# A transformer block in fp32 by split matmuls: seven-product pairs in every FFN group, three hidden tiles parked in DRAM, and the delta rule's norm weight moved to the split

## The chip, the cores and the metric

The kernel runs on one core of one Trainium2 chip, as one launch. The metric is the device time of a launch in microseconds (us), the median of three runs. TensorE is called PE below, VectorE DVE, ScalarE ACT, GpSimd POOL and SyncE SP.

## The reference

One hybrid transformer block on 256 tokens of width 2048, in fp32:

```python
proj = x @ w_in                                   # q,k,v of both branches, z, gates
o_a = gated_delta_rule_chunked(...)               # 8 heads of 128
o_a = o_a * rsqrt(mean(o_a**2) + eps) * gdn_norm_w * silu(z)
o_b = dsa_sparse_attention(...)
merged = sigmoid(gate_a) * (o_a @ w_branch_a) + sigmoid(gate_b) * (o_b @ w_branch_b)
x = layer_norm(ALPHA * x + merged @ w_out, ln1_g, ln1_b)
h_gate, h_up = split(x @ w_ffn_in)                # 2 x 5632 columns
x = layer_norm(ALPHA * x + (silu(h_gate) * h_up) @ w_ffn_out, ln2_g, ln2_b)
```

`gdn_norm_w` has 128 entries, one for each position within a head.

## The kernel before

**Split matmuls.** Each fp32 matrix is split into a rounded part `hi` and a rest `lo`, and a product is three matmuls, hi*hi + hi*lo + lo*hi (`mm3`). Weights arrive as 512 KB chunks of 128 x 1024: SP loads a chunk into one of four `raw` tiles, ACT makes `hi` (line 80), DVE makes `lo` (line 82), and PE uses both (`chunk`). There are four tiles each of `raw`, `hi` and `lo`; a load, a cast or a subtraction waits until its tile was given free.

**Pairs.** In the gate groups, the FFN groups and the output projection, the contraction goes in pairs `q` of two chunks (256 rows), against 1024 columns and both token blocks. A plain pair (`plain_pair`) is 8 block products, 24 matmuls of 512 columns. A seven-product pair (`seven_pair`) multiplies the 2 x 2 blocks by a scheme with 7 products, so it is 21 matmuls. It needs sums of weight blocks (`wt`, lines 248 to 252) with their own hi and lo (`thi`, `tlo`, lines 237 and 238), sums of the activations (`forms`), and a second bank of four PSUM tiles (`wbank`), which is joined to the first one later (`sums_chain`, `seven_chain`). `GQ`, `FQ` and `WQ` are the tables of which pairs are of seven products: `GQ` for the four gate groups, `FQ` for the FFN groups, `WQ` for the two column halves of the output projection.

**FFN.** Group 0 (`wfi`) is done plainly. Groups 1 to 10 (8 pairs each) give 512 hidden features each; `hidden_chain` forms silu(gate)*up, transposes it on PE (line 1150) and splits it into the tiles `hH[i]`, `hL[i]`. Where the output projection treats its pairs by seven products, the chain also makes their `forms` and writes them to DRAM (`d_g`). A chain is a generator that yields the number of ticks (half pairs) until its next step; `tick()` runs after each half pair, so the yields set where its matmuls stand in PE's order.

**Order.** PE and SP execute in program order (`manual_schedule`), with weight chunks moved ahead by `LEAD`. DVE, ACT and POOL are put in order by the tile scheduler, by priority; each engine then executes in that fixed order, so an instruction that waits holds up all behind it. The tiles `hH[7]` to `hH[10]` and `hL[7]` to `hL[10]` lie where the FFN's `f_wraw`, `f_wt`, `f_thi` and `f_tlo` are, and the activations' forms lie in the place of `x1`. So groups 8 to 10, during which those tiles are filled and `x1` is read back, are plain.

**Output projection.** `group(0, ...)` and `group(1, ...)` go over 22 pairs each. At pair 2 of group 0 the last chains are run out (`finish`), and the pools for the seven-product tiles (`wraw`, `wt`, `thi`, `tlo`, `gt`) are opened where the activations lay.

**Other places.** `out_gate_chain` multiplies silu(z) by the norm weight on POOL (line 837). `block_xs` for `wbb` (branch b) takes its PSUM tiles from `acc`, as does the gate group after it.

Of the kernel before, what the change touches and what calls it, by code (L numbers as in the profile page):

```python
# [52 lines left out]
def block_kernel(ctx: ExitStack, tc: tile.TileContext, xT, x, cpack, onehot, relb, convw, alog, dtb, gnw,  # L53
# [941 lines left out]
    hH, hL = [], []  # L995

    def h_tiles(pool, n):
        for _ in range(n):
            i = len(hH)
            hH.append(pool.tile([P, 4, S], F32R, name=f"hH{i}", tag=f"hH{i}"))  # L1000
            hL.append(pool.tile([P, 4, S], F32R, name=f"hL{i}", tag=f"hL{i}"))

    h_tiles(hp_, 5)
# [101 lines left out]
    h_tiles(hp2, 2)  # L1105
# [27 lines left out]
    def hidden_chain(i, bank, v, std):  # L1133

        if v is None:
            v = [fv() for _ in range(4)]
            for tb in range(NTB):
                nc.scalar.activation(v[2 * tb], bank[2 * tb], AF.Silu)
                nc.vector.tensor_mul(v[2 * tb + 1], bank[2 * tb + 1], v[2 * tb])
        else:  # L1140
            for tb in range(NTB):
                g, u = v[2 * tb:2 * tb + 2]
                nc.vector.tensor_tensor(g, bank[2 * tb], g, op=OP.subtract if tb else OP.add)
                nc.scalar.activation(g, g, AF.Silu)
                nc.vector.tensor_add(u, bank[2 * tb + 1], u)
            for tb in range(NTB):
                g, u = v[2 * tb:2 * tb + 2]
                nc.vector.tensor_mul(u, u, g)
        yield 4 if i < NG else 2
        a = [quad(lambda o, f: nc.tensor.transpose(o, v[2 * tb + 1][:, f * P:(f + 1) * P], ident), std)  # L1150
             for tb in range(NTB)]
        ps = [p for p in (2 * i, 2 * i + 1) if p in WALL]
# [20 lines left out]
    for i in range(1, NG + 1):  # L1173
        if i > 7:
            h_tiles(hp2, 1)
        if i == 8:
            x1 = [rp.tile([P, D], F32, name=f"x1_{tb}", tag=f"x1_{tb}") for tb in range(NTB)]
            for tb in range(NTB):
                nc.gpsimd.dma_start(x1[tb], d_x1[tb])
# [160 lines left out]
def _arrays(i):  # L1340
# [13 lines left out]
    def paired(m):  # L1354
# [63 lines left out]
```

## Time and profile before

| | |
|---|---|
| median of 3 runs | 1478.28 us (1476.67 to 1478.88) |
| profiled execution, its own time | 1477.79 us |
| span of its instructions | 1476.0 us |
| PE busy | 1459.3 us (99%), 7191 matmuls |
| DVE busy | 1146.1 us (78%) |
| ACT busy | 766.5 us (52%) |
| POOL busy | 52.6 us (4%) |
| moved by DMA | 307.59 MB, 208 GB/s over the span |
| granted clock of TensorE | 0.998 |

The span runs from the first to the last instruction of the profiled execution; the time has 1.8 us around it. Matmuls overlap in the pipeline: a row's duration is longer than the distance to the next row's start, and the cost of one is that distance.

### The profile page before, as it was taken

What the parts mean: (1) busy time and instruction counts of PE and PEld (TensorE: products, weight loads), DVE (VectorE), ACT (ScalarE), POOL (GpSimd) and SP (SyncE); (2) the same over time, 40 slices, a digit from 0 to 9 for tenths busy, and PEclk for the clock granted to TensorE, in tenths of its full rate; (3) what the DMA queues carried; (4) which work ended last, traced back from release to release, by engine and by line L of the source; (5) the groups of instructions that cost most, each with busy time, mean ns of one, the idle gap of its engine ahead of it and who ended that gap; (6) DMA issues with size and microseconds to landing.
All of it is one profiled execution on the core that took longest, in us unless ns stands there. A gap on an engine that the chain in (4) does not pass through costs nothing.

```text
span 1476.0 us, 19311 instructions
## 1 busy us (share of the span) xinstructions
PE 1459.3 (99%) x7191; PEld 1226.0 (83%) x7191; DVE 1146.1 (78%) x1534; ACT 766.5 (52%) x932; POOL 52.6 (4%) x63
## 2 busy tenths in 40 slices
PE   9999999999999999999999999999999999999996
PEld 9888888888888888888878888888888888888885
DVE  6798985468488678776676889988895556999896
ACT  6765443446466456543445556555554444664560
POOL 0001010020010000000000000000000000000000
PEclk9999999999999999999999999999999999999999
DMA  8656584545556665558656566666676666877862
GB/s 295 193 153 198 179 193 152 158 129 158 168 185 215 199 213 187 186 185 299 227 187 207 184 234 216 218 216 236 227 255 220 200 209 224 303 262 244 322 217 87
DMA packets 92398, 307.59 MB, mean 208 GB/s; under 512 B 16448, under 2 KB 17512, under 8 KB 91280
## 3 DMA queue, kind: packets, MB, share of 16 engines
q1 hardware_dynamic: 80592, 283.36, 58.9%
q0 software_dynamic: 4672, 20.65, 4.0%
q10 hardware_dynamic: 7040, 2.36, 0.7%
q8 instruction: 56, 0.92, 0.3%
q14 instruction: 38, 0.31, 0.1%
HBM read 292.50 MB, written 13.83 MB: 208 GB/s over the span
## 4 chain that ended last, share of the span: by engine, by line
PE 95%; DVE 2%; DMA 1%; ACT 1%; issue 1%; SPq 0%; POOLq 0%; DVEq 0%; ACTq 0%
PE acc L142 10%; PE acc L205 10%; PE acc L206 10%; PE acc L204 10%; PE aux L205 8%; PE aux L206 8%; PE aux L204 8%; PE acc L164 7%; PE acc L163 7%; PE acc L162 7%; PE acc L145 5%; PE aux L669 1%; DMA raw<-in_win_dram 1%; DVE lo L82 1%; ACT hi L80 1%
## 5 line engine op out<-in xcount | busy, mean ns | idle before, releaser
L82 DVE TENSOR_TENSOR lo<-raw,hi 128x1024 fp32r<-128x1024 f32 (+1 forms) x421 | 514.8, 1228 | 240.2 <-ACT hi L80 237.1
L80 ACT CAST hi<-raw 128x1024 fp32r<-128x1024 f32 (+1 forms) x421 | 437.7, 1046 | 483.6 <-PE acc L164 125.3
L142 PE MATMUL acc<-X,hi 128*128 128x512 f32 x640 | 203.7, 400 | 0.0
L204 PE MATMUL acc<-hi,X 128*128 128x512 f32 x388 | 151.6, 391 | 0.5 <-DVE s_vT L971 0.5
L206 PE MATMUL acc<-hi,X 128*128 128x512 f32 x388 | 151.0, 389 | 0.0
L205 PE MATMUL acc<-lo,X 128*128 128x512 f32 x388 | 151.0, 389 | 0.0
L145 PEld LDWEIGHTS acc<-X,lo 128*128 128x128 f32 x640 | 120.2, 188 | 28.3
L204 PE MATMUL aux<-hi,X 128*128 128x512 f32 x340 | 132.9, 391 | 0.0
L206 PE MATMUL aux<-hi,X 128*128 128x512 f32 x340 | 132.4, 389 | 0.0
L205 PE MATMUL aux<-lo,X 128*128 128x512 f32 x340 | 132.3, 389 | 0.0
L162 PE MATMUL acc<-hi,X 128*128 128x512 f32 x320 | 127.1, 397 | 0.0
L145 PE MATMUL acc<-X,lo 128*128 128x256 f32 x640 | 126.0, 278 | 0.0
L164 PE MATMUL acc<-hi,X 128*128 128x512 f32 x320 | 124.7, 390 | 0.0
L163 PE MATMUL acc<-lo,X 128*128 128x512 f32 x320 | 124.6, 389 | 0.0
L142 PEld LDWEIGHTS acc<-X,hi 128*128 128x128 f32 x640 | 97.5, 189 | 2.0 <-ACT hi L80 0.7
L204 PEld LDWEIGHTS acc<-hi,X 128*128 128x128 f32 x388 | 72.8, 188 | 15.9 <-DVE s_vT L971 1.0
L206 PEld LDWEIGHTS acc<-hi,X 128*128 128x128 f32 x388 | 72.8, 188 | 15.1
L205 PEld LDWEIGHTS acc<-lo,X 128*128 128x128 f32 x388 | 72.9, 188 | 15.0
L206 PEld LDWEIGHTS aux<-hi,X 128*128 128x128 f32 x340 | 63.8, 188 | 13.3
L205 PEld LDWEIGHTS aux<-lo,X 128*128 128x128 f32 x340 | 63.8, 188 | 13.1
L204 PEld LDWEIGHTS aux<-hi,X 128*128 128x128 f32 x340 | 63.8, 188 | 13.0
L164 PEld LDWEIGHTS acc<-hi,X 128*128 128x128 f32 x320 | 60.1, 188 | 12.7
(518 smaller groups left out, 2562.6 us busy)
## 6 DMA issues: line engine op xcount, KB each, us to landing
raw<-in_wfg_dram SPq DMA_DIRECT2D x143, 512.0 KB, 4.0
raw<-in_wws_dram SPq DMA_DIRECT2D x80, 512.0 KB, 3.8
raw<-in_wfo_dram SPq DMA_DIRECT2D x69, 512.0 KB, 4.6
raw<-in_wgt_dram SPq DMA_DIRECT2D x53, 512.0 KB, 3.6
raw<-in_win_dram SPq DMA_DIRECT2D x37, 512.0 KB, 3.7
raw<-in_wo_dram SPq DMA_DIRECT2D x32, 512.0 KB, 4.3
wraw<-in_wfo_dram SPq DMA_DIRECT2D x19, 512.0 KB, 5.0
gt<-d_g SPq DMA_DIRECT2D x19, 512.0 KB, 6.6
```

The lines of the kernel that those rows point to most:

```text
L80: nc.scalar.copy(hi, raw)
L82: nc.vector.tensor_sub(lo, raw, hi.bitcast(F32))
L142: nc.tensor.matmul(pss[c], hv[:, kk, cs[c]], X2[k // 4][:, k % 4], start=(k == 0), stop=False, skip_group_check=True)
L145: nc.tensor.matmul(pss[c][:, :S], lv[:, kk, cs[c]], xh[:, k, :], start=False, stop=(k == KT - 1), skip_group_check=True)
L162: nc.tensor.matmul(ps, xh, hv[:, kk], start=(k == 0), stop=False)
L163: nc.tensor.matmul(ps, xh, lv[:, kk], start=False, stop=False)
L164: nc.tensor.matmul(ps, xl, hv[:, kk], start=False, stop=(k == 2 * n - 1))
L204: nc.tensor.matmul(o, sh, hi, start=first, stop=False)
L205: nc.tensor.matmul(o, sh, lo, start=False, stop=False)
L206: nc.tensor.matmul(o, sl, hi, start=False, stop=last)
L669: nc.tensor.matmul(o, l, r, start=True, stop=True)
```

## The change

- The tables: `FQ` gives each FFN group but the first three seven-product pairs, (2, 4, 6), and all of the groups 1 to 10; `GQ` gives the first gate group a third one, pair 2; `WQ` has 10 and 8 pairs in place of 11 and 8, at other places.
- The hidden tiles of groups 0, 1 and 2 go through one pair of tiles (`pass`) to DRAM (`d_h`) and are read back by SP during group 0 of the output projection (`FETCH`), whose rows of `wfo` are put in another order, groups 3 to 10 first, then 1, 2 and 0. `x1` is written to DRAM by SP in place of POOL, somewhat later, and read back by SP at pairs 15 to 18 in place of group 8 of the FFN.
- `hidden_chain` copies both transposed tiles to SBUF on ACT, splits from there, and waits three ticks in all groups (before: four, and two in the last).
- The norm weight is a [128, 1] operand, applied where the transposed delta-rule output is split; the multiplication on POOL is gone.
- The last `wbb` block takes PSUM tiles of `aux`.

```diff
-WQ = ((2, 4, 6, 8, 9, 11, 13, 14, 16, 18, 19), (3, 5, 7, 8, 10, 12, 13, 15))
-GQ = ((4, 6), (2, 4, 6), (2, 4, 6), (2, 4, 6))
+WQ = ((2, 4, 6, 8, 9, 11, 12, 16, 17, 19), (3, 5, 7, 8, 10, 12, 13, 16))
+GQ = ((2, 4, 6),) * 4
-FQ = {1: (4, 6), 2: (4, 6), 3: (3, 4, 6), 4: (4, 6), 5: (3, 4, 6), 6: (4, 6), 7: (3, 4, 6)}
+FQ = ((4, 6), *[(2, 4, 6)] * 9)
+OUT_AT = (8, 9, 10)
+FETCH = (5, 7, 9, 10, 13, 14)
...
-        nc.gpsimd.tensor_tensor(s_rv.rearrange("p a h d -> p (a h) d"), s_rv.rearrange("p a h d -> p (a h) d"),
-                                bc(gnw_t[:, None, :], [P, NTB * H, P]), op=OP.mult)
...
-                split(oh_[:, hs, tb * P:(tb + 1) * P], ol_[:, hs, tb * P:(tb + 1) * P], a)
+                nc.scalar.activation(oh, a, AF.Copy, scale=gnw_t[:, 0:1])
+                nc.vector.scalar_tensor_tensor(ol, a, gnw_t[:, 0:1], oh.bitcast(F32), op0=OP.mult, op1=OP.subtract)
...
-        for tb, ps in enumerate(block_xs([wbb[j, k] for k in range(4)], oh_, ol_)):
+        for tb, ps in enumerate(block_xs([wbb[j, k] for k in range(4)], oh_, ol_, ps_aux if j == 3 else ps_acc)):
...
+    def put_out(i, hl):
+        for j, t in enumerate(hl):
+            nc.gpsimd.dma_start(d_h[i, j], t.rearrange("p k t -> p (k t)").bitcast(F32))
+    def fetch(i, j):
+        t = (hH, hL)[j][i]
+        nc.sync.dma_start(t.rearrange("p k t -> p (k t)").bitcast(F32), d_h[i, j])
...
-        nc.gpsimd.dma_start(d_x1[tb], x1[tb])
...
     def f_forms_chain():
         yield "x1"
+        for tb in range(NTB):
+            yield 2
+            nc.sync.dma_start(d_x1[tb], x1[tb])
...
-        yield 4 if i < NG else 2
+        yield 3
         a = [quad(lambda o, f: nc.tensor.transpose(o, v[2 * tb + 1][:, f * P:(f + 1) * P], ident), std)
              for tb in range(NTB)]
-        ps = [p for p in (2 * i, 2 * i + 1) if p in WALL]
-        if ps:
-            hq = fp.tile([P, 512], F32, name="hq", tag="hq", bufs=1)
-            nc.scalar.copy(hq, a[1])
+        hq = v[::2]
+        with tc.high_priority(offset=LEAD // 2):
+            for tb in range(NTB):
+                nc.scalar.copy(hq[tb], a[tb])
...
-            split(hH[i][:, :, ts], hL[i][:, :, ts], v4(a[tb]))
+            split(hl[0][:, :, ts], hl[1][:, :, ts], v4(hq[tb]))
+        if i < 3:
+            put_out(at, hl)
...
+            if not g and q in FETCH:
+                fetch(OUT_AT[0] + FETCH.index(q) // 2, FETCH.index(q) % 2)
+            if not g and 15 <= q < 19:
+                c, tb = divmod(q - 15, 2)
+                cs = slice(c * 1024, c * 1024 + 1024)
+                nc.sync.dma_start(x1[tb][:, cs], d_x1[tb, :, cs])
```

How the order of instructions moves, at three places. Lines in the changed kernel's rows are some two to twenty higher.

ACT's order at the start of the output projection, before: `hH_10448` is the tile of the last FFN group (its input `acc` are the transposes), `wraw` the first seven-product pair's weights.

```order
L1138 ACTIVATE v<-acc 128x512 x2
L80 CAST hi<-raw 128x1024
L195 CAST hH_10448<-acc 128x4x128 x2
L237 CAST hi<-wraw 128x1024
L237 CAST hi<-raw 128x512
L237 CAST thi<-wt 128x1024
```

The same place in the changed kernel.

```order
L1158 ACTIVATE v<-v 128x512
L82 CAST hi<-raw 128x1024
L1158 ACTIVATE v<-v 128x512
L1169 COPY v<-acc 128x512 x2
L197 CAST hH_10512<-v 128x4x128 x2
L239 CAST hi<-wraw 128x1024
L239 CAST hi<-raw 128x512
L239 CAST thi<-wt 128x1024
```

Before the first cast of `wraw` stand four instructions that depend on the transposes, where there were two; the transposes themselves stand behind 36 matmuls of the output projection in PE's order, where it was 24.

DVE's order in an FFN group with three seven-product pairs, before, around pairs 3 and 4: `fg` and `gs` are the forms of the group before, `f_wt` and `f_tlo` the weight sums.

```order
L238 TENSOR_TENSOR lo<-f_wraw,hi 128x1024
L252 TENSOR_TENSOR f_wt<-f_wt,raw 128x512
L269 TENSOR_TENSOR fg<-hq 128x2x128
L238 TENSOR_TENSOR lo<-raw,hi 128x512
L270 TENSOR_TENSOR fg<-acc,fg 128x2x128
L271 TENSOR_TENSOR fg<-hq,acc 128x2x128
L272 TENSOR_TENSOR fg<-acc,fg 128x2x128
L82 TENSOR_TENSOR lo<-raw,hi 128x1024 x2
L196 TENSOR_TENSOR gs<-fg,gs 128x2x512
L238 TENSOR_TENSOR f_tlo<-f_wt,f_thi 128x1024 x2
```

The same place in the changed kernel, around pair 4.

```order
L240 TENSOR_TENSOR lo<-f_wraw,hi 128x1024
L198 TENSOR_TENSOR hL_6126<-v,hH_6125 128x4x128
L271 TENSOR_TENSOR fg<-v 128x2x128
L240 TENSOR_TENSOR lo<-raw,hi 128x512
L272 TENSOR_TENSOR fg<-v,fg 128x2x128
L273 TENSOR_TENSOR fg<-v 128x2x128
L253 TENSOR_TENSOR f_wt<-f_wt,f_wraw 128x512
L274 TENSOR_TENSOR fg<-v,fg 128x2x128
L254 TENSOR_TENSOR f_wt<-f_wt,raw 128x512
L240 TENSOR_TENSOR f_tlo<-f_wt,f_thi 128x1024
L198 TENSOR_TENSOR gs<-fg,gs 128x2x512
L240 TENSOR_TENSOR f_tlo<-f_wt,f_thi 128x1024
```

The first `f_tlo` of a pair now stands ahead of `gs` and of the plain chunks' `lo`, and a plain pair lies between any two seven-product pairs.

SP's order in group 0 of the output projection, changed kernel, pairs 15 to 18 (before, the same queue had only `wraw`, `raw` and `gt` here): `x_0`, `x_1` are the two token blocks of `x1`.

```order
L1280 DMA x_0_10620<-d_x_6110 128x1024
L80 DMA raw<-in_wfo_dram 128x1024 x2
L1280 DMA x_1_10621<-d_x_6110 128x1024
L233 DMA wraw<-in_wfo_dram 128x1024
L235 DMA raw<-in_wfo_dram 128x1024
L1217 DMA gt<-d_g 128x1024
L1280 DMA x_0_10620<-d_x_6110 128x1024
L233 DMA wraw<-in_wfo_dram 128x1024
L235 DMA raw<-in_wfo_dram 128x1024
L1217 DMA gt<-d_g 128x1024
L1280 DMA x_1_10621<-d_x_6110 128x1024
L80 DMA raw<-in_wfo_dram 128x1024 x2
```

Four loads of `x1` stand among the weights' loads here, and six of `d_h` do so at the pairs of `FETCH`.

## Rows read from the trace of the kernel before

**Rows 1.** The page: busy time of each engine, and the chain that ended last.

```profile
PE 1459.3 (99%) x7191; PEld 1226.0 (83%) x7191; DVE 1146.1 (78%) x1534; ACT 766.5 (52%) x932; POOL 52.6 (4%) x63
PE 95%; DVE 2%; DMA 1%; ACT 1%; issue 1%; SPq 0%; POOLq 0%; DVEq 0%; ACTq 0%
```

**Rows 2.** Timeline of PE, output projection's start: start, duration, instruction, idle before.

```profile
1235.31 0.39 PE L204 MATMUL aux<-hi,hH 128*128 128x512 f32 x1
...
1240.52 0.40 PE L206 MATMUL aux<-hi,hL 128*128 128x512 f32 x1
1240.76 1.04 PE L1150 MATMUL acc<-ident,v 128*128 128x128 f32 x8
...
1250.52 0.39 PE L204 MATMUL acc<-thi,gt 128*128 128x512 f32 x1
1251.16 0.50 PE L205 MATMUL acc<-tlo,gt 128*128 128x512 f32 x1 [0.25 <-DVE tlo L238]
```

**Rows 3.** Stretches between transposes: length, PE, PEld, DVE, ACT, POOL, clock, DMA, GB/s.

```profile
855.30:898.40 43.10, 43.10 (x197) 35.78 (x196) 39.31 (x47) 25.65 (x30) 1.05 (x2) 1.00 0.68 231
898.40:941.20 42.80, 42.65 (x193) 35.05 (x192) 38.89 (x46) 24.39 (x29) 1.06 (x2) 1.00 0.65 210
1113.10:1157.50 44.40, 44.40 (x202) 36.85 (x201) 24.56 (x25) 20.26 (x22) 1.05 (x2) 1.00 0.67 214
```

**Rows 4.** The same by whole groups: group 3 (three seven-product pairs), group 4 (two).

```profile
887.50:930.40 42.90, 42.75 (x192) 35.12 (x192) 41.28 (x49) 25.61 (x30) 1.06 (x2) 1.00 0.64 209
930.40:973.40 43.00, 43.00 (x195) 35.72 (x194) 36.91 (x44) 24.46 (x28) 1.05 (x2) 1.00 0.70 231
```

**Rows 5.** Timeline of DVE in group 3.

```profile
898.61 1.22 DVE L238 TENSOR_TENSOR f_tlo<-f_wt,f_thi 128x1024 fp32r<-128x1024 f32 x1
899.75 0.68 DVE L238 TENSOR_TENSOR lo<-raw,hi 128x512 fp32r<-128x512 f32 x1
900.35 1.22 DVE L248 TENSOR_TENSOR f_wt<-f_wraw,raw 128x1024 f32<-128x1024 f32 x1
...
906.42 0.41 DVE L271 TENSOR_TENSOR fg<-hq,acc 128x256 f32<-128x256 f32 x1
906.75 0.41 DVE L272 TENSOR_TENSOR fg<-acc,fg 128x256 f32<-128x256 f32 x1
```

**Rows 6.** Timeline of PE in group 3, pair 4.

```profile
911.38 0.39 PE L204 MATMUL acc<-f_thi,f_form 128*128 128x512 f32 x1
911.91 0.50 PE L205 MATMUL acc<-f_tlo,f_form 128*128 128x512 f32 x1
```

**Rows 7.** Timeline of PE, from branch b to the third gate group.

```profile
533.62 0.39 PE L206 MATMUL acc<-hi,X 128*128 128x512 f32 x1
534.56 0.50 PE L204 MATMUL acc<-hi,X 128*128 128x512 f32 x1 [0.55 <-DVE s_vT L971]
```

**Rows 8.** Timeline of ACT, output projection's start.

```profile
1241.39 1.08 ACT L195 CAST hH<-acc 128x512 fp32r<-128x512 f32 x2 [4.83 <-PE acc L1150]
1242.35 1.06 ACT L237 CAST hi<-wraw 128x1024 fp32r<-128x1024 f32 x1
```

**Rows 9.** Timeline of DVE, output projection's start.

```profile
1243.45 1.23 DVE L238 TENSOR_TENSOR lo<-wraw,hi 128x1024 fp32r<-128x1024 f32 x1
...
1249.88 1.23 DVE L238 TENSOR_TENSOR tlo<-wt,thi 128x1024 fp32r<-128x1024 f32 x1
```

**Rows 10.** Busy time by stretch of the output projection; the last two columns are DMA.

```profile
1260.00:1270.00 10.00, 10.00 (x46) 8.29 (x45) 9.83 (x10) 5.49 (x7) 0.00 (x0) 1.00 0.95 338
...
1370.00:1380.00 10.00, 10.00 (x45) 8.29 (x45) 8.28 (x10) 6.14 (x7) 1.06 (x2) 1.00 1.00 370
```

**Rows 11.** Waits from 1235 us on: in total, times, longest.

```profile
DVE wt L248 <- DMA raw<-in_wfo_dram: 3.5, 4, 1.9
```

**Rows 12.** Timeline of POOL, first gate group.

```profile
410.34 4.63 POOL L837 TENSOR_TENSOR s_rv<-s_rv,gnw 128x2048 f32<-128x2048 f32 x1 [83.01 <-ACT s_rv L836]
```

**Rows 13.** Busy time around that instruction.

```profile
400.00:425.00 25.00, 25.00 (x112) 20.70 (x111) 17.45 (x19) 13.95 (x14) 4.63 (x1) 1.00 0.62 198
```

More of the change, by code (lines that the diff above doesn't have):

```diff
@@ L891, in forms_chain @@
     def forms_chain(room):
-        for q in (4, 6, 2):
+        for q in (2, 4, 6):
             yield 1
@@ L994, in block_kernel, with h_tile, passing @@
     hp_ = fh.enter_context(tc.tile_pool(name="hp", bufs=1, side="left", reuse_waits="tile"))
[L995 to L1003, printed above, removed]
+    hH, hL = [None] * (FT // 4), [None] * (FT // 4)
+    def h_tile(pool, i):
+        hH[i], hL[i] = (pool.tile([P, 4, S], F32R, name=f"{hl}{i}", tag=f"{hl}{i}") for hl in ("hH", "hL"))
+    d_h = dr.tile([FT // 4, 2, P, 1024], F32, name="d_h")
+    def passing():
+        return [hp_.tile([P, 4, S], F32R, name="pass", tag=f"{hl}0") for hl in ("hH", "hL")]
+    def put_out(i, hl):
[4 more added lines that the diff above has]
+        nc.sync.dma_start(t.rearrange("p k t -> p (k t)").bitcast(F32), d_h[i, j])
+    h_first = passing()
+    for i in range(1, 5):
+        h_tile(hp_, i)
     l1 = ExitStack()
@@ L1098, in h_chain @@
         fs = slice(2 * j, 2 * j + 2)
-        split(hH[0][:, fs, ts], hL[0][:, fs, ts], a[:, :2 * P].rearrange("p (k t) -> p k t", k=2))
+        split(h_first[0][:, fs, ts], h_first[1][:, fs, ts], a[:, :2 * P].rearrange("p (k t) -> p k t", k=2))
+        if j and tb:
+            put_out(OUT_AT[2], h_first)
     block_xs_stag([wfi[0, k] for k in range(8)], xh, xl, ex,
@@ L1104, in block_kernel @@
     hp2 = fh.enter_context(tc.tile_pool(name="hp2", bufs=1, side="left", reuse_waits="tile"))
-    h_tiles(hp2, 2)
+    for i in (5, 6):
+        h_tile(hp2, i)
     f_home = {}
@@ L1120, in f_forms_chain @@
         yield "x1"
+        for tb in range(NTB):
+            yield 2
+            nc.sync.dma_start(d_x1[tb], x1[tb])
         t = [rp.tile([P, 2, 2, 4, P], F32R, name="f_form", tag=f"x1_{tb}") for tb in range(NTB)]
-        for i, q in enumerate((4, 6, 3)):
+        for i, q in enumerate((4, 2, 6)):
             yield 1
@@ L1133, in hidden_chain @@
     def hidden_chain(i, bank, v, std):
[L1135 to L1148, printed above, removed]
-        yield 4 if i < NG else 2
+        for tb in range(NTB):
+            g, u = v[2 * tb:2 * tb + 2]
+            nc.vector.tensor_tensor(g, bank[2 * tb], g, op=OP.subtract if tb else OP.add)
+            nc.scalar.activation(g, g, AF.Silu)
+            nc.vector.tensor_add(u, bank[2 * tb + 1], u)
+        for tb in range(NTB):
+            g, u = v[2 * tb:2 * tb + 2]
+            nc.vector.tensor_mul(u, u, g)
+        yield 3
         a = [quad(lambda o, f: nc.tensor.transpose(o, v[2 * tb + 1][:, f * P:(f + 1) * P], ident), std)
              for tb in range(NTB)]
-        ps = [p for p in (2 * i, 2 * i + 1) if p in WALL]
-        if ps:
-            hq = fp.tile([P, 512], F32, name="hq", tag="hq", bufs=1)
-            nc.scalar.copy(hq, a[1])
+        hq = v[::2]
+        with tc.high_priority(offset=LEAD // 2):
+            for tb in range(NTB):
+                nc.scalar.copy(hq[tb], a[tb])
+        at = OUT_AT[i - 1] if i < 3 else i - 3
+        if i == 3:
+            h_tile(hp_, 0)
+        hl = passing() if i < 3 else (hH[at], hL[at])
         for tb in range(NTB):
             ts = slice(tb * P, tb * P + P)
-            split(hH[i][:, :, ts], hL[i][:, :, ts], v4(a[tb]))
+            split(hl[0][:, :, ts], hl[1][:, :, ts], v4(hq[tb]))
+        if i < 3:
+            put_out(at, hl)
+        ps = [p for p in (2 * at, 2 * at + 1) if p in WALL]
         if ps:
@@ L1165, in hidden_chain @@
             gi = [g[:, :, j] for j in range(4)]
-            forms(gi, pv(a[0], 0), pv(hq, 0), pv(a[0], 1), pv(hq, 1))
+            forms(gi, pv(hq[0], 0), pv(hq[1], 0), pv(hq[0], 1), pv(hq[1], 1))
             gs = fp.tile([P, 2, 2, 4, P], F32R, name="gs", tag="gs", bufs=1)[:, :n]
@@ L1173, in block_kernel @@
     for i in range(1, NG + 1):
[L1174 to L1179, printed above, removed]
         std, shared = (ps_aux, ps_acc) if i % 2 else (ps_acc, ps_aux)
@@ L1185, in places @@
             return sums
-        bank = x_group(wfg[i - 1], FQ.get(i, ()), std, shared, f_form, fhome, places)
-        start(hidden_chain(i, bank, sums or None, std), at_once=True)
-    h_tiles(hp2, 1)
+        bank = x_group(wfg[i - 1], FQ[i - 1], std, shared, f_form, fhome, places)
+        if i == NG:
+            h_tile(hp2, 7)
+        start(hidden_chain(i, bank, sums, std), at_once=True)
     hh_, hl_ = KV(hH), KV(hL)
@@ L1245, in group @@
                 finish()
+                for i in OUT_AT:
+                    h_tile(hp2, i)
+                for tb in range(NTB):
+                    x1[tb] = rp.tile([P, D], F32, name=f"x1_{tb}", tag=f"x1_{tb}")
                 xs_.close()
@@ L1393, in _arrays @@
         "wfg": paired(wf1),
-        "wfo": paired(np.asarray(i["w_ffn_out"])[0]),
+        "wfo": paired(np.asarray(i["w_ffn_out"])[0].reshape(FT // 4, 512, D)[[*range(3, FT // 4), 1, 2, 0]].reshape(D_FF, D)),
         "ln1g": ca(np.asarray(i["ln1_g"])[0]),
```

11 lines of the change are left out of this document (6 added, 5 removed).

## The prediction

> **What bounds the kernel now.** I read the page first: PE is busy for 99% of the span and makes up 95% of the chain that ended last [rows 1]. A busy PE proves little here, since its rows overlap, so I looked next at the distance between matmuls: 23 steps from 1235.31 to 1240.52 are 0.227 us each [rows 2], though a row lasts 0.39. PE starts one matmul every 0.227 us nearly without a gap, so the time is the number of matmuls times 0.227 plus the few gaps. Third come the stretches of the FFN: a group of plain pairs takes 44.40 us, which is 192 matmuls (43.6) and 0.8 for eight transposes; one with two seven-product pairs takes 43.10, as 186 matmuls should; one with three takes 42.80 where 183 should take 42.36 [rows 3]. So 0.44 us is lost there, and the timeline shows where: an L205 waits for the `lo` of a weight sum, 0.53 after the matmul ahead in place of 0.23 [rows 6]. DVE, which makes these, is 78% busy on average but 41.28 of 42.90 us in such a group [rows 4]. The FFN is bound by PE, with DVE close behind.
>
> **The change part by part.**
>
> *Matmuls.* A seven-product pair has 21 matmuls where a plain one has 24. The gates gain one such pair, the FFN 12 (from 17 to 29), the output projection loses one (19 to 18): 12 more, 36 matmuls fewer, 36 x 0.227 = 8.2 us. No other work on PE is added; the transposes stay.
>
> *Is DVE fast enough for three in nine groups?* Its rows follow each other by 1.14 us (1024 elements), 0.60 (512) and 0.33 (256) [rows 5]. A steady group of the changed kernel has 48 instructions on DVE: 23 of 1024 (three seven-product pairs of 4, five plain ones of 2, the split of the forms), 21 of 512 and 4 of 256: 26.2 + 12.6 + 1.3 = 40.1 us, against 42.4 on PE. It fits by 2.3 us. Before, the stall came from pairs 3 and 4 being neighbours (two times 6.4 us of DVE work against 4.8 of PE) with the hidden chain's forms between. Now a plain pair follows each (6.4 + 2.3 = 8.7 against 10.2), and the two `f_tlo` no longer stand behind `gs` and two `lo`. I walked the new order of one group with these durations: the last weight sum of pair 2 is ready about 12.6 us after the group's start and needed at 15.3; for pairs 4 and 6 the margins are about 2.5 and 4. I take no stall in these groups, so the three old ones (groups 3, 5 and 7) go too: -1.3. The extra copies of `hidden_chain` are on ACT, 25.6 of 42.9 us busy [rows 4]; that engine waits for free tiles, not for time. If this cover is gone, it is the second rival.
>
> *Gates.* The third gate group waits now for the last branch-b tile: 0.94 from 533.62 to 534.56 where 0.23 is due [rows 7]. With `aux` tiles for that block it need not: -0.7. The forms for the new pair 2 of the first group are the first made instead of the last, well ahead. POOL's 4.63 us go, but PE was busy for all of 25.00 us around it [rows 12, 13], so that is worth nothing; what replaces it, four casts and four subtractions of 512 elements, only changes form. I put it at 0, from -0.3 to 0.5.
>
> *Start of the output projection.* This is the term against. ACT executes in order, and there its first cast of `wraw` stands behind what depends on the last group's transposes. Before: the projection starts at 1235.31, the transposes come 24 matmuls later, at 1240.76 [rows 2], two casts follow at 1241.39, and the cast of `wraw` at 1242.35 [rows 8], so one such cast takes 0.48. From there DVE's work runs through to the last `tlo`, 1249.88 + 1.23 [rows 9], and PE, due at 1250.75, starts at 1251.16 [rows 2]: 0.4 late already. Now the transposes come after 36 matmuls (12 x 0.227 = 2.7 later) and four instructions stand ahead instead of two (2 x 0.48 = 1.0): everything behind is 3.7 later, with the same matmuls ahead on PE. Nothing else can fill the gap, since all of PE is in order: +3.7. From below it is 0, if the scheduler's order mattered less than I read; from above 4.5, if the SBUF casts are slower than those from PSUM.
>
> *The parked tiles.* Writing them is 3 MB on POOL's queue in groups where the DMA is at 0.64 to 0.70 [rows 4]: 0. The two writes of `x1`, now on SP's queue, delay the chunks of `wfi` behind them by a transfer each; those are loaded some four chunks ahead: 0. Reading them back puts ten loads of 512 KB into SP's queue at pairs 5 to 18 of group 0. Pairs 5 to 19 then move 14 chunks for plain pairs, 24 for the eight others and these ten, 48 x 0.524 = 25.2 MB, in 7 x 5.45 + 8 x 4.77 = 76.3 us of PE: 330 GB/s. The trace shows 338 GB/s at a share of 0.95 and 370 at 1.00 [rows 10], so it fits, narrowly. Waits for weights cost DVE 3.5 us in the whole projection before [rows 11], and PE none of it. From below the cost is 0; from above, if each of the ten delays what DVE needs by its own transfer (0.524 / 338 GB/s = 1.55 us), 15.5. I take 0.7, near the lower end, as the loads are mostly issued when the next pair's tiles are not yet free anyway.
>
> The Trainium skill's page "DMA: Bandwidth & Descriptors", section "Where 436 GB/s comes from", gives about 358 GB/s as the limit from HBM to one core and 435 for the fabric. The stretch at 370 lies between the two, so this trace doesn't confirm the lower one exactly. By 358, pairs 16 and 17, with 8 loads in 9.5 us, would fall 2.2 us behind and an estimate of the DMA term would be up to 2.2; by 435 it would be 0.
>
> *Sum.* 1477.79 (the profiled execution's own time) - 8.2 - 1.3 - 0.7 + 3.7 + 0.7 = 1472.0. That execution lies 0.5 below the median of 1478.28, so I predict 1472.5.
>
> **The rivals.**
>
> *No penalty at the start of the output projection*: the 3.7 are absent, and it is 1468.8. For it: three ticks were chosen for all groups alike, where the chain could run earlier by priority. Against it: the order of ACT is fixed, and `wraw`, loaded from 1235 on, evidently waited for the casts of `hH`. 10%.
>
> *DVE stalls stay in the FFN*: nine groups lose the 0.44 that each group of three lost so far, 4.0 us in place of 0, and it is 1476.5. For it: DVE was 41.28 of 42.90 us busy, and so far a group with two such pairs (36.91 of 43.00) followed, in which it could catch up [rows 4]; now none does. Against it: 40.1 us by its rows, and the better order. 15%.
>
> *The loads come late* (the side of slower): in group 0 of the output projection, DVE has no idle time to lose (9.83 of 10 us [rows 10]), so a weight that lands late passes through to PE one for one. It decides once more than about 1 us is lost before pair 9, the margin that remains there after the late start. With the full 1.55 for each of the ten loads it is 1472.5 - 0.7 + 15.5 = 1487. For it: 0.95 of the DMA is used already at 1260 to 1270. Against it: pairs 13 to 15 are plain, and the loads are asked for several pairs ahead. 8%.
>
> *Nothing comes of it*: the gaps move and eat the 8 us elsewhere, 1478. For it: 99% busy PE says little. Against it: the spacing by stretches follows the number of matmuls closely [rows 3]. 5%.
>
> **How the numbers follow.** The forecast has 62%. Its own range is 1470.5 to 1475: no DMA cost and a smaller penalty on one side, 2 us of DMA or stalls on the other. The whole range, 1469 to 1477.5, takes in the first two rivals and leaves out the late loads and most of no change. A measurement tells a change from none at about 0.2%, 3 us: faster is below 1475.3. That holds for nearly all of the forecast (0.59), the first rival (0.10) and a third of the second (0.05): 0.74. Within it are the rest of these and no change: 0.18. Slower, above 1481.2: 0.08.
>
> **What would show it.** After, PE has 36 matmuls fewer at the same 0.227 spacing, and the FFN's stretches between transposes are 42.4 us from group 2 on. If they are 42.8, the second rival holds. In the output projection's first seven-product pair, PE's gaps sum to about 4 us (0.4 before) with DVE's `lo` and `tlo` as releasers, and ACT's cast of `wraw` starts 10.7 us after the projection does (7.0 before). Waits of DVE on `raw` in group 0 stay below 6 us; if they are 10 or more with gaps on PE at pairs 8 to 17, it is the late loads. The forecast is wrong if the time is below 1470 or above 1475.

## The result and the profile after

| | before | changed |
|---|---|---|
| median | 1477.91 us (4 runs, 1476.67 to 1478.88) | 1470.09 us (4 runs, 1469.85 to 1470.48) |
| profiled execution, its own time | 1477.79 us | 1469.85 us |
| span | 1476.0 us | 1468.1 us |
| matmuls on PE | 7191 | 7155 |

The ratio is 0.9948, with a 95% interval of 0.9931 to 0.9965: 7.8 us faster. The forecast was 1472.5, with its own range from 1470.5 to 1475, so the time is 0.4 below that and inside the whole range (1469 to 1477.5).

The page of the changed kernel: busy time and the chain that ended last, as [rows 1].

```profile
PE 1452.0 (99%) x7155; PEld 1219.9 (83%) x7155; DVE 1202.0 (82%) x1613; ACT 792.0 (54%) x972; POOL 47.9 (3%) x62
...
PE 97%; DVE 1%; DMA 1%; ACT 0%; issue 0%; SPq 0%; POOLq 0%; DVEq 0%; ACTq 0%
```

There are 36 matmuls fewer and 56 us more work on DVE. PE's share of the chain rose by two points: less of the time is waiting than before.

The FFN's stretches from one set of transposes to the next, with the columns of [rows 3]: length, PE, PEld, DVE, ACT, POOL, clock, DMA.

```profile
850.80:893.20 42.40, 42.40 (x193) 35.19 (x192) 41.02 (x49) 26.28 (x31) 2.12 (x4) 1.00 0.71 248
893.20:935.60 42.40, 42.40 (x193) 35.18 (x192) 39.74 (x49) 26.04 (x32) 1.60 (x3) 1.00 0.68 235
...
1147.50:1189.90 42.40, 42.40 (x192) 35.18 (x191) 40.99 (x49) 26.27 (x31) 1.05 (x2) 1.00 0.65 224
```

All nine stretches are 42.37 to 42.41 us long, where a group with three such pairs took 42.8 before [rows 3]. DVE is busy for 40 to 41 of the 42.4 us, but no L207 waits for a `tlo` as in [rows 6].

The start of the output projection, which is at 1224.14 here. First PE, the place of [rows 2].

```profile
1224.14 0.39 PE L206 MATMUL aux<-hi,hH 128*128 128x512 f32 x1
...
1232.30 1.04 PE L1164 MATMUL acc<-ident,v 128*128 128x128 f32 x8
...
1236.11 0.49 PE L206 MATMUL acc<-hi,hH 128*128 128x512 f32 x1
1237.37 0.50 PE L207 MATMUL acc<-lo,hH 128*128 128x512 f32 x1 [0.77 <-DVE lo L240]
...
1239.67 0.42 PE L206 MATMUL acc<-thi,gt 128*128 128x512 f32 x1
1240.84 0.50 PE L207 MATMUL acc<-tlo,gt 128*128 128x512 f32 x1 [0.76 <-DVE tlo L240]
...
1242.53 0.50 PE L206 MATMUL acc<-thi,gt 128*128 128x512 f32 x1 [0.29 <-ACT thi L239]
1243.79 0.50 PE L207 MATMUL acc<-tlo,gt 128*128 128x512 f32 x1 [0.76 <-DVE tlo L240]
```

Then ACT there, as [rows 8].

```profile
1232.99 1.07 ACT L1169 COPY v<-acc 128x512 f32<-128x512 f32 x2 [7.00 <-PE acc L1164]
1233.95 1.15 ACT L197 CAST hH<-v 128x512 fp32r<-128x512 f32 x2
1234.99 1.07 ACT L239 CAST hi<-wraw 128x1024 fp32r<-128x1024 f32 x1
```

The transposes come 1232.30 - 1224.14 = 8.16 us after the start (36 x 0.227), and the cast of `wraw` 10.85 us after it (7.04 before). The distances from one matmul's start to the next (the steps) in the first seven-product pair exceed 0.227 by 4.3 us in sum, against 0.5 before; this sum is called PE's excess below. From 1244.2 to 1319 no step exceeds 0.227 by 0.1.

Busy time by stretch where the ten loads stand, as [rows 10]; the last two columns are DMA's share and GB/s.

```profile
1250.00:1260.00 10.00, 10.00 (x46) 8.29 (x45) 9.04 (x10) 5.56 (x7) 0.00 (x0) 1.00 0.95 352
1260.00:1270.00 10.00, 10.00 (x45) 8.28 (x45) 9.57 (x10) 6.56 (x8) 0.00 (x0) 1.00 1.01 393
...
1300.00:1310.00 10.00, 10.00 (x46) 8.29 (x45) 7.01 (x8) 3.79 (x4) 0.00 (x0) 1.00 1.01 402
```

PE is busy throughout, and DVE's waits for weights from 1224 on, as [rows 11], have become shorter: in total, times, longest.

```profile
DVE wt L250 <- DMA raw<-in_wfo_dram: 2.2, 2, 1.7
```

Two differences were in no term of the forecast. The first is at the transposes of `x1` (L944 before, L946 after), here PE before the change:

```profile
763.84 0.39 PE L164 MATMUL acc<-hi,X 128*128 128x512 f32 x1
765.02 0.63 PE L944 MATMUL aux<-ident,x 128*128 128x128 f32 x4 [0.79 <-issue]
```

and after it:

```profile
763.22 0.39 PE L166 MATMUL acc<-hi,X 128*128 128x512 f32 x1
763.60 0.63 PE L946 MATMUL aux<-ident,x 128*128 128x128 f32 x4
```

PE waited there for nothing that the trace shows ("issue"), and 0.8 us of that step are gone (1.0 with the second such step). Much of this need not be the change's doing: in e10 below, whose instructions are those of the kernel before up to here, the step is 0.67 and not 1.18.

```profile
764.48 0.63 PE L944 MATMUL aux<-ident,x 128*128 128x128 f32 x4 [0.28 <-issue]
```

In the eight traces with the changed kernel's instructions up to here it is 0.38 to 0.67. The other difference is the end of the program. The last instruction of DVE, before:

```profile
1470.07 1.41 DVE L1034 SCALAR_TENSOR_TENSOR x<-x,rs,ln 128x512 f32<-128x512 f32 x2
```

and after:

```profile
1463.43 1.41 DVE L1049 SCALAR_TENSOR_TENSOR x<-x,rs,ln 128x512 f32<-128x512 f32 x2
```

From its end to the end of the span it is 4.5 us before and 3.2 after.

### The profile page after: what moved, and what is told of

It reads as the page before. It is cut to its first block, busy times and chain, and to the rows that moved or that the text cites. A ratio compares the mean times of both kernels' runs of the same rounds, so it can differ in the third digit from the quotient of the medians.

```text
span 1468.1 us, 19377 instructions
## 1 busy us (share of the span) xinstructions
PE 1452.0 (99%) x7155; PEld 1219.9 (83%) x7155; DVE 1202.0 (82%) x1613; ACT 792.0 (54%) x972; POOL 47.9 (3%) x62
## 3 DMA queue, kind: packets, MB, share of 16 engines
q10 hardware_dynamic: 7040, 2.36, 0.7%
## 4 chain that ended last, share of the span: by engine, by line
PE 97%; DVE 1%; DMA 1%; ACT 0%; issue 0%; SPq 0%; POOLq 0%; DVEq 0%; ACTq 0%
PE acc L144 10%; PE acc L207 9%; PE acc L208 9%; PE acc L206 9%; PE aux L206 9%; PE aux L208 9%; PE aux L207 9%; PE acc L164 7%; PE acc L166 7%; PE acc L165 7%; PE acc L147 5%; PE aux L671 1%; DMA raw<-in_win_dram 1%; PE aux L946 0%; DMA s_vT<-in_xT_dram 0%; PE aux L825 0%
## 5 line engine op out<-in xcount | busy, mean ns | idle before, releaser
L82 ACT CAST hi<-raw 128x1024 fp32r<-128x1024 f32 (+1 forms) x397 | 412.1, 1045 | 406.6 <-PE acc L166 120.8
L84 DVE TENSOR_TENSOR lo<-raw,hi 128x1024 fp32r<-128x1024 f32 (+1 forms) x397 | 481.0, 1220 | 176.6 <-ACT hi L82 173.5
L206 PE MATMUL aux<-hi,X 128*128 128x512 f32 x329 | 128.6, 391 | 0.0
L208 PE MATMUL aux<-hi,X 128*128 128x512 f32 x329 | 128.1, 389 | 0.0
L207 PE MATMUL aux<-lo,X 128*128 128x512 f32 x329 | 128.0, 389 | 0.0
L164 PE MATMUL acc<-hi,X 128*128 128x512 f32 x320 | 127.1, 397 | 0.0
L206 PE MATMUL acc<-hi,X 128*128 128x512 f32 x321 | 125.4, 391 | 0.0
L208 PE MATMUL acc<-hi,X 128*128 128x512 f32 x321 | 125.0, 389 | 0.0
L207 PE MATMUL acc<-lo,X 128*128 128x512 f32 x321 | 124.9, 389 | 0.0
L166 PE MATMUL acc<-hi,X 128*128 128x512 f32 x320 | 124.7, 390 | 0.0
L165 PE MATMUL acc<-lo,X 128*128 128x512 f32 x320 | 124.6, 389 | 0.0
L239 ACT CAST f_thi<-f_wt 128x1024 fp32r<-128x1024 f32 x58 | 61.1, 1054 | 43.0 <-DVE f_wt L250 24.6
L208 PEld LDWEIGHTS aux<-hi,X 128*128 128x128 f32 x329 | 61.8, 188 | 12.9
L206 PEld LDWEIGHTS aux<-hi,X 128*128 128x128 f32 x329 | 61.8, 188 | 12.8 <-DVE ol__105 L851 0.3
L207 PEld LDWEIGHTS aux<-lo,X 128*128 128x128 f32 x329 | 61.8, 188 | 12.7
L240 DVE TENSOR_TENSOR f_tlo<-f_wt,f_thi 128x1024 fp32r<-128x1024 f32 x58 | 70.5, 1220 | 1.7 <-ACT f_thi L239 1.2
L208 PEld LDWEIGHTS acc<-hi,X 128*128 128x128 f32 x321 | 60.2, 188 | 12.6
L166 PEld LDWEIGHTS acc<-hi,X 128*128 128x128 f32 x320 | 60.1, 188 | 12.7
```

What stands on the lines that cost most here:

```text
L82: nc.scalar.copy(hi, raw)
L84: nc.vector.tensor_sub(lo, raw, hi.bitcast(F32))
L164: nc.tensor.matmul(ps, xh, hv[:, kk], start=(k == 0), stop=False)
L165: nc.tensor.matmul(ps, xh, lv[:, kk], start=False, stop=False)
L166: nc.tensor.matmul(ps, xl, hv[:, kk], start=False, stop=(k == 2 * n - 1))
L206: nc.tensor.matmul(o, sh, hi, start=first, stop=False)
```

## The experiments

**The start of the output projection: e1, e2, e3.** Three runs undo the two parts of the term against, the later transposes (e1), the copies on ACT (e2), and both (e3).

```diff
-        yield 3
+        yield 3 if i < NG else 2
```

> The changed kernel, but the last FFN group's chain yields 2 before its transposes (24 matmuls of the output projection ahead of them in place of 36). Theory A (ACT's fixed order: the first cast of wraw stands behind the copies and casts of the last group, and PE's gaps in the first seven-product pair follow the time of that cast one for one): the transposes come 12 matmuls = 2.7 us earlier, the cast of wraw starts 8.1 us after the projection does (10.85 in the changed kernel), PE's gaps sum to 1.5 us (4.3), the time is 1467.4. Rival B (the gap is set by the load of wraw, or by DVE's own work, not by the transposes): the cast stays near 10.8, 1470.1.

```diff
+        if i == NG:
+            hq = a
+        else:
+            ...   (the copies on ACT)
```

> The changed kernel, but the last FFN group is split straight from PSUM, without the two copies on ACT; the transposes stay after 36 matmuls. Theory A: two instructions less ahead of the cast of wraw, which starts 9.9 us after the projection (10.85), PE's gaps 3.3 us, 1469.1. Rival B: no change, 1470.1.

> Both edits: yield 2 and the split straight from PSUM in the last group. Theory A: the cast of wraw starts 7.1 us after the projection, as in the kernel before, PE's gaps there are 0.5 us, the time is 1470.1 - 3.8 = 1466.3: the two edits add up. Rival B: 1470.1. A mixed case (the transposes wait for their input once they come early, DVE's last v is ready 4.4 us after the projection's start) would show as a gap on PE ahead of the transposes.

The cast of `wraw` is counted from the projection's first matmul, which is at 1223.74 in e1, 1223.36 in e2 and 1224.45 in e3.

| | cast of `wraw` after the start | PE's excess | median |
|---|---|---|---|
| changed kernel | 10.85 us | 4.3 us | 1470.09 |
| e1, yield 2 | 8.13 | 1.6 | 1467.49 (5 runs, 1466.49 to 1467.86) |
| e2, no copies | 9.77 | 3.2 | 1468.41 (5 runs, 1467.87 to 1469.23) |
| e3, both | 7.05 | 0.5 | 1466.33 (4 runs, 1465.73 to 1466.51) |

ACT's cast of `wraw` in e1, e2 and e3:

```profile
1231.87 1.07 ACT L239 CAST hi<-wraw 128x1024 fp32r<-128x1024 f32 x1
...
1233.13 1.06 ACT L239 CAST hi<-wraw 128x1024 fp32r<-128x1024 f32 x1
...
1231.50 1.06 ACT L239 CAST hi<-wraw 128x1024 fp32r<-128x1024 f32 x1
```

PE in e1, where its waits are:

```profile
1239.42 0.50 PE L206 MATMUL acc<-thi,gt 128*128 128x512 f32 x1 [0.26 <-ACT thi L239]
1240.68 0.50 PE L207 MATMUL acc<-tlo,gt 128*128 128x512 f32 x1 [0.76 <-DVE tlo L240]
```

PE in e3:

```profile
1239.66 0.39 PE L206 MATMUL acc<-thi,gt 128*128 128x512 f32 x1
1240.30 0.50 PE L207 MATMUL acc<-tlo,gt 128*128 128x512 f32 x1 [0.25 <-DVE tlo L240]
```

What is left in e3 is the wait of the kernel before, 0.64 from one start to the next [rows 2]. The excess falls by 2.7, 1.1 and 3.8 us, as the cast comes 2.7, 1.1 and 3.8 earlier: one for one, and the two edits add up. Theory A holds, to 0.2 us in each trace. e2's time fell by 0.6 more than its excess; in its profiled execution the projection already starts 0.8 earlier than in the changed kernel, ahead of the edited place. e3 is faster than both kernels, with a ratio to the kernel before of 0.992 (0.9906 to 0.9933).

**Neighbouring pairs: e4.**

```diff
-FQ = ((4, 6), *[(2, 4, 6)] * 9)
+FQ = ((4, 6), *[(3, 4, 6)] * 9)
```

> The changed kernel with the three seven-product pairs of the FFN groups at (3, 4, 6), two of them neighbours, in place of (2, 4, 6); as many matmuls, as many instructions on DVE. Theory (it is the neighbours that stall PE, 0.3 us of gap and 0.1 behind it in each group, as in groups 3, 5 and 7 of the kernel before; DVE's total does not): nine groups lose 0.4 each, 1470.1 + 3.6 = 1473.7. Rival (the total of DVE's work decides, or the late gs ahead of f_tlo, which the other order of the chain has mended): 1470.1.

It took 1471.58 us (5 runs, 1470.91 to 1472.21), +1.5. One of its stretches:

```profile
1021.50:1064.10 42.60, 42.60 (x192) 35.11 (x191) 41.04 (x49) 26.11 (x31) 1.06 (x2) 1.00 0.67 220
```

Seven of the nine are 42.59 to 42.74 long and two 42.4, together 1.7 more than in the changed kernel. So neighbours cost something, but 0.2 per group and not 0.44: the other half of the old stall is gone even with neighbours. What else differs in these groups is the changed hidden chain (its copies, and its other order on DVE); that it is this, and which part of it, was not tried. Neither side was right alone.

**The number of matmuls: e5.**

```diff
-FQ = ((4, 6), *[(2, 4, 6)] * 9)
+FQ = ((4, 6),) * 10
```

> The changed kernel with two seven-product pairs, (4, 6), in all ten FFN groups: 9 pairs less, 27 matmuls more. Theory (PE starts one matmul every 0.227 us, and the number of them is the whole of the FFN's time): 1470.1 + 6.1 = 1476.2, with no other change. Rival (DVE, now 82% busy, already costs something in the groups with three): less than +6.1, as DVE is relieved of 9 x 4.0 us; with 0.2 us per group, 1474.4.

It took 1476.87 us (11 runs, 1476.27 to 1479.10), +6.8. A stretch of it:

```profile
894.90:938.00 43.10, 43.10 (x196) 35.75 (x195) 36.10 (x43) 24.38 (x29) 1.59 (x3) 1.00 0.70 232
```

All nine are 43.05 to 43.09, so the first to the last transposes take 387.61 us against 381.49: 6.12 for 27 matmuls, 0.227 each. DVE has 5 us less to do in a group and PE gains nothing from it. In the traces the rest lies ahead of these nine stretches, which begin 1.1 later (851.95 against 850.81) though nothing was edited there.

**The loads: e6 and e9.**

```diff
+                for _ in range(2):
                     fetch(...)
...
+                for _ in range(2):
                     nc.sync.dma_start(x1[tb][:, cs], d_x1[tb, :, cs])
```

> The changed kernel with each of the ten loads of the parked tiles and of x1 issued twice, one behind the other: 20 loads of 512 KB in group 0 of the output projection in place of 10. Theory (the ten loads fit, but narrowly: the DMA moves at most 370 GB/s): pairs 5 to 19 would move 58 x 0.524 = 30.4 MB in 76.3 us, 398 GB/s; at 370 that is 82 us, so PE loses 3 to 6 us to late weights, 1473 to 1476. Rival (far from the limit, or the loads wait in the queue while nothing needs them): no change, 1470.1. Upper rival (each load passes through): 15.5, 1485.6.

It took 1490.17 us (4 runs, 1489.56 to 1490.63): 20 more than the changed kernel, above even the upper rival. SP's queue shows that this run measures something else.

```profile
1256.35 8.80 SPq L1014 DMA_DIRECT2D hH<-d_h  x2
1265.26 0.37 SPq L233 DMA_DIRECT2D wraw<-in_wfo_dram  x1
```

The second load of a tile is issued only 6 to 11 us after the first, into the same tile, and all that is behind it in SP's queue waits as long. So it tells of a wait in the queue and not of the DMA's rate. e9 asks again, with loads that wait for no other load:

```diff
+MORE = (5, 6, 7, 8, 10, 11, 12, 13)
...
+            if not g and q in MORE:
+                c, tb = divmod(MORE.index(q) % 4, 2)
+                cs = slice(c * 1024, c * 1024 + 1024)
+                nc.sync.dma_start(x1[tb][:, cs], d_x1[tb, :, cs])
```

> The changed kernel with eight more loads of 512 KB in SP's queue in group 0 of the output projection (quarters of x1, at pairs 5, 6, 7, 8, 10, 11, 12 and 13, into tiles nobody reads before their own load at pairs 15 to 18), none of which waits for another load. In the run with each load issued twice, the second of a pair was issued 6 to 11 us after the first, which held the whole queue; that run told of a wait in the queue, not of the DMA. Theory (it is the wait that cost 20 us there; the DMA itself has some room): pairs 5 to 14 move 39 x 0.524 = 20.4 MB in 51 us, 400 GB/s where 370 to 379 were seen, so 4 us late at most, less what the four raw tiles hold ahead: 1470 to 1473. Rival (the DMA is at its limit with the ten loads, and each further one costs its own 1.4 us): 1470.1 + 11 = 1481.

It took 1472.02 us (5 runs, 1470.63 to 1473.65), +1.9. The stretches:

```profile
1250.00:1260.00 10.00, 10.00 (x46) 8.29 (x45) 9.13 (x10) 5.56 (x7) 0.00 (x0) 1.00 1.03 416
1260.00:1270.00 10.00, 10.00 (x46) 8.29 (x45) 8.72 (x9) 5.67 (x7) 0.00 (x0) 1.00 1.03 408
1270.00:1280.00 10.00, 10.00 (x46) 8.29 (x45) 9.59 (x10) 6.93 (x9) 0.00 (x0) 1.00 1.03 409
1280.00:1290.00 10.00, 10.00 (x46) 8.29 (x45) 8.80 (x11) 3.94 (x5) 0.00 (x0) 1.00 1.02 408
1290.00:1300.00 10.00, 9.48 (x42) 7.47 (x42) 9.33 (x9) 6.14 (x7) 0.00 (x0) 1.00 0.64 211
```

For 40 us the DMA moves 408 to 416 GB/s while PE runs on, and only then come three waits (at 1293.7, 1320.2 and 1322.5), by which steps are 0.5 to 0.8 us too long. Eight more loads cost 2 us in all. The ten alone left no step of PE too long where they stand, as shown above, so they cost none, and what the DMA can move lies well above the 370 of [rows 10].

**The norm weight: e7.**

```diff
-        nc.gpsimd.tensor_tensor(s_rv..., bc(gnw_t[:, None, :], [P, NTB * H, P]), op=OP.mult)
...
-                split(oh_[...], ol_[...], a)
+                nc.scalar.activation(oh, a, AF.Copy, scale=gnw_t[:, 0:1])
+                nc.vector.scalar_tensor_tensor(ol, a, gnw_t[:, 0:1], oh.bitcast(F32), op0=OP.mult, op1=OP.subtract)
```

> The kernel before with one edit: the norm weight as a [128, 1] operand at the split of the transposed delta-rule output, the multiplication on POOL gone. Theory (PE was busy throughout beside it, so it is worth nothing): 1477.9, PE's rows from 400 to 425 as before. Rival (DVE instructions beside POOL's were slow, 5.96 us for two, and their end mattered later): up to 0.8 us faster, 1477.1.

It took 1476.84 us (11 runs, 1476.10 to 1480.92), and the kernel before 1478.45 (27 runs); the ratio is 0.9991 (0.9982 to 1.0000), so a gain of 1 us is likely but not certain. In its trace the third gate group takes 0.5 longer (from its first matmul to L944's first transposes, those of `s_kT`, 102.52, before 102.05), mostly the wait of [rows 7], now 1.27 from start to start. That the norm weight lengthens it is not shown: in e11 below, with the same split, this step is 0.63, and in e12, with the multiplication on POOL, it is 0.78. The rows of that wait, and two from the second column half of the output projection:

```profile
534.73 0.39 PE L206 MATMUL acc<-hi,X 128*128 128x512 f32 x1
536.00 0.50 PE L204 MATMUL acc<-hi,X 128*128 128x512 f32 x1 [0.89 <-DVE s_vT L971]
...
1418.81 0.39 PE L204 MATMUL acc<-hi,hH 128*128 128x512 f32 x1
1420.28 0.50 PE L205 MATMUL acc<-lo,hH 128*128 128x512 f32 x1 [1.08 <-DVE lo L238]
```

From the last DVE instruction to the end it is 3.4 us instead of 4.5. This profiled execution took 1480.92, the longest of its runs: PE's steps are 3.3 us too long at three waits for `lo` and `tlo` between 1394 and 1424, in the second column half; in the kernel before's own trace they are 0.2 too long there.

**The aux tiles: e8.**

```diff
-        for tb, ps in enumerate(block_xs([...], oh_, ol_)):
+        for tb, ps in enumerate(block_xs([...], oh_, ol_, ps_aux if j == 3 else ps_acc)):
```

> The kernel before with one edit: the last block of branch b takes its PSUM tiles from aux. Theory (the third gate group no longer waits for the last multiplication of branch b): the step of 0.94 us ahead of that group becomes 0.23, -0.7 to -0.8. Rival (part of it comes back as a wait in that group's first seven-product pair, 0.28 us, as the changed kernel shows at 547.57): -0.4 to -0.5. In total 1477.2 to 1477.5.

1477.74 us (11 runs, 1476.89 to 1480.28), ratio 0.9997 (0.9989 to 1.0006): by time nothing can be said. In the trace the wait at the third gate group's start is gone (every step 0.23), which makes 0.8 us, and from its first matmul to L944's first transposes it takes 101.56 instead of 102.05: -0.5. The rival holds: 0.3 comes back where the group's first seven-product pair begins. There the loading of PE's weights (PEld) waits for the split of the delta-rule output, `ol`, which reads the `aux` tiles that the transposes had filled. First e8, then the changed kernel at the same place; the kernel before shows no such wait there.

```profile
PEld aux L204 <- DVE ol__105 L196: 0.3, 1, 0.3
PEld aux L206 <- DVE ol__105 L851: 0.7, 2, 0.4
```

Twenty-five steps there (in the changed kernel from 543.63 to 549.01) take 4.79 us before, 4.83 in e7, 5.10 in e8 and 5.38 in the changed kernel (5.15 to 5.44 in the eight traces that have its instructions up to there).

**The scatter of the kernel before: e10.**

```diff
-(3, 5, 7, 8, 10, 12, 13, 15))
+(3, 5, 7, 8, 10, 12, 13, 16))
```

> The kernel before with one number changed: in group 1 of the output projection the last seven-product pair is 16 in place of 15; as many matmuls. Theory (some of the changed kernel's gain beyond the forecast is that with pairs 12, 13 and 15 DVE falls behind there: in one profiled run of the kernel before with the norm weight's edit PE waited 3.3 us for lo and tlo at these pairs, in the kernel before's own 0.2): the times scatter less (the kernel before has 1476.5 to 1481.1) and the median falls by about 1 us, to 1477. Rival (the scatter is elsewhere): 1478.2, as wide as before.

1477.60 us (11 runs, 1476.96 to 1478.76), the kernel before 1478.72 (15 runs, 1476.98 to 1481.38); ratio 0.9994 (0.9986 to 1.0003). The scatter is narrower, and the median 1.1 lower, but the interval holds 1. It is in the direction of the theory and not shown.

**The end of the program, and the place of the tiles: e11 and e12.** Both add a small tile and an instruction on POOL, e11 to e7's kernel, e12 to the kernel before.

```diff
+        nc.gpsimd.tensor_tensor(sm.tile([P, 1], F32, name="gsq"), gnw_t, gnw_t, op=OP.mult)
```

> The kernel before with the norm weight's edit (as in the run with that alone) and one small instruction more on POOL, [128, 1] times [128, 1] into a tile that nobody reads, so that POOL again has as many instructions as in the kernel before. What is asked: the end of the program. The three kernels with the multiplication on POOL (before, the aux tiles alone, pair 16 in place of 15) show 4.5 us from the last DVE instruction's end to the end of the span and one packet of the instruction queue in the last 9 us; the nine without it show 3.1 to 3.4 and no such packet. Theory (the number of instructions on POOL decides, since it sets where its code is fetched in pieces): 4.5 us and one packet again, about 1.1 us longer than with the norm weight's edit alone, near 1477.9. Rival (it is the multiplication itself, or the DVE and ACT instructions of the edit): 3.1 to 3.4 us, no packet, 1476.8.

```diff
+        nc.gpsimd.memset(sm.tile([P, 1], F32, name="gsq"), 0.0)
```

> The kernel before with a tile of [128, 1] more in the pool of small tiles, and one memset of it on POOL near the start; the other engines' orders are those of the kernel before. The run with the norm weight's edit and a small POOL instruction was 9.6 us slower than the run with the edit alone; its trace shows no more waits, but matmuls 0.2275 to 0.232 us apart where 0.2267 were usual. Its new tile also moved whatever lies behind the small tiles in SBUF. Theory (it is the place of the tiles in SBUF that widens the steps): here too, about 8 to 9 us slower than the kernel before, 1487, with the same wider steps. Rival (the steps came from something else in that run, the instruction on POOL or its wait for the norm weight's load): 1478.5 with steps of 0.2267.

e11 took 1486.49 us (5 runs, 1485.96 to 1487.41), e12 1487.00 (5 runs, 1485.61 to 1487.89): 8 to 10 slower, which e12's theory forecast and e11's did not. On the end of the program e11's theory fell: its tail is 3.4 us with no packet of the instruction queue in the last 9 us, while e12, with the multiplication still on POOL, has 4.5 and such a packet, as the three others with it. So the tail goes with the norm weight's edit. Whether it is the multiplication that is gone or the new split that does it, and how, stays open: every trace without the one has the other. Busy times in e12 over 100 us of the output projection:

```profile
1300.00:1400.00 100.00, 100.00 (x433) 81.04 (x432) 92.15 (x101) 54.84 (x58) 2.15 (x4) 1.00 0.76 264
```

The kernel before:

```profile
1300.00:1400.00 100.00, 100.00 (x443) 82.78 (x442) 91.79 (x101) 54.51 (x59) 2.14 (x4) 1.00 0.78 273
```

Ten matmuls fewer fit into 100 us at the same granted clock and with PE never idle. The mean step in these 100 us is 0.2318 in e12 and in e11, against 0.2267 before. Both runs have the new tile and the new instruction, and none has one of them alone. The instruction is over at 2.6 us in e12 and at 23.6 us in e11, and the steps are too wide as late as 1400, so it is not its running that widens them. That leaves the place of the tiles behind the new one as the likelier cause, by argument and not by a run.

## Why the prediction was right, point by point

- *The time:* right, with some luck. It lies 2.4 below the forecast and 0.1 above 1470, below which the prediction called itself wrong, and two of the four runs are below that. By the time alone the first rival, no penalty at the output projection, would be nearer (1468.8, which the whole range, from 1469, just leaves out, although the prediction says that it takes it in). The traces and e1 to e3 decide: the penalty is there, and the time came back at places that no term had.
- *Bound by PE, 0.227 a matmul:* right. e5 gives 6.12 us for 27 matmuls.
- *36 matmuls, -8.2:* right by the count and the step. The first two gate groups gained 0.5 of their 0.7, as their steps average 0.2272 where it was 0.2267.
- *No stall with three seven-product pairs, -1.3:* right, the nine stretches are 42.4. The reason given first, the neighbours, was half of it: e4 shows that they cost 0.2 per group; the other part of the old 0.44 is gone even with neighbours.
- *Third gate group, -0.7, and the norm weight, 0:* the step that failed in size. The wait is gone, but from the first matmul of that group to L944's first transposes the changed kernel is 0.2 shorter, not 0.7 (0.1 to 0.4 in the eight traces that have its instructions up to there). PE comes 0.8 earlier to the group's first seven-product pair and loses 0.6 of it there (0.4 to 0.65 in these eight), waiting for the split of the delta-rule output. The forecast stopped at the wait that goes and did not look for the next one. It also called what replaces the multiplication a change of form, but that is the instruction waited for: a pair of it on DVE takes 1.40 us in the changed kernel and 1.28 before, and in the one trace with the old form (e8) 0.3 is lost. How much of the 0.6 is the new form's is open within that scatter.
- *Start of the output projection, +3.7:* right, 3.8 by the trace, with the cast at 10.85 us where 10.7 was forecast, and taken apart by e1 to e3 into 2.7 for the twelve matmuls and 1.1 for the two copies.
- *The loads, +0.7:* 0 by the trace, and eight more of them cost 2 us (e9). Of the figures weighed from the Trainium skill's page "DMA: Bandwidth & Descriptors", section "Where 436 GB/s comes from", the lower one, 358, is no limit for this one core, by 40 us at 408 to 416 GB/s in e9; the upper one, 435, was not reached.
- *What was not forecast:* -1.0 at the transposes of `x1` and -1.3 at the end. The first is a wait for nothing shown, which varies by 0.5 between the kernel before and e10 though their instructions are the same up to there; no run ties it to an edit. The second goes with the norm weight's edit in all traces (4.5 us in the four with POOL's multiplication, 3.1 to 3.4 in the ten without).

The sum by the traces is -8.2 + 0.2 (first gate groups) - 1.4 (the three old stalls) - 0.2 (third gate group) + 3.8 - 1.0 - 1.3 = -8.1, and the profiled executions differ by 7.9. Against the forecast's -5.8, 0.7 are the loads and 2.3 the two unforeseen places, less 0.7 in the gates. It is a sum over one execution of each kernel: the eight traces with the changed kernel's instructions reach the first gate group between 404.8 and 406.1, so a few tenths in a term of it can be chance.

## What to carry to other kernels

Where the engine that bounds is fed in a fixed order, price a delayed step by following the one engine whose queue it stands in: here two numbers, 12 matmuls and two instructions, gave a loss of 3.7 us, where the trace has 3.8 and e3 gets it back. A wait that is taken away is worth only what the next wait on that engine leaves of it: 0.8 became 0.2 in the third gate group. A copy that costs nothing in nine groups can cost something in the tenth, whose successor needs the engine at once. And a test of a transfer's cost must not make the transfers wait for each other.

## What was not expected of the hardware

- A tile of 128 x 1 more in the pool of small tiles, with one short POOL instruction that writes it, costs 8 to 9 us (e12, ratio 1.0059, 1.0045 to 1.0073): the granted clock is the same, and from 1300 to 1400 PE never waits, but the matmuls there are 0.2318 us apart in place of 0.2267. That it is the place of the tiles is not shown, and which tile's place would matter was not tried.
- The DMA held 408 to 416 GB/s for 40 us while DVE, ACT and PE worked (e9).
- Beside POOL's multiplication, which runs from 410.34 to 414.97 [rows 12], two subtractions of DVE took 5.96 us in the kernel before; in e7, without it, two of the same form took 2.36. PE had no use for the difference.

```profile
411.23 5.96 DVE L82 TENSOR_TENSOR lo<-raw,hi 128x1024 fp32r<-128x1024 f32 x2 [3.41 <-ACT hi L80]
...
412.47 2.36 DVE L82 TENSOR_TENSOR lo<-raw,hi 128x1024 fp32r<-128x1024 f32 x2
```

- In e6, after a wait of 3 us on PE, the granted clock was 0.66 over the stretch from 1310 to 1320, and matmuls were 0.43 us apart in place of 0.227, as at the lower of the two levels (1.2 GHz). Several waits of about 0.8 from 1326 to 1341 left it at 1.00. PE's wait and the stretch in e6:

```profile
1313.56 0.80 PE L206 MATMUL aux<-hi,hH 128*128 128x512 f32 x1 [3.03 <-ACT hi L82]
...
1310.00:1320.00 10.00, 6.50 (x16) 4.52 (x15) 2.45 (x2) 2.09 (x2) 0.00 (x0) 0.66 0.78 293
```
